# Grouped 3x3 convolution: the distance at which input loads are issued, and wait instructions early on two engines

## The chip, the cores and the metric

The kernel runs on one core of one Trainium2 chip. The metric is the device time of one execution in microseconds (us). Eight executions of the kernel before took 125.8 to 126.14 us, median 125.95. The profile is one further execution of its own; its time stands in the table below.

## The reference

Sixteen images of 64 channels and 64 x 64 pixels are convolved with 3 x 3 filters in 8 groups (8 input and 16 output channels each), with zero padding. Everything is float32 in HBM.

```python
batch, c_in, h, w, c_out, k, groups = 16, 64, 64, 64, 128, 3, 8
x_pad = np.pad(x, ((0, 0), (0, 0), (pad, pad), (pad, pad)))
for g in range(groups):
    for b, co, ci, kh, kw in ...:
        output[b, g * 16 + co] += weight[g * 16 + co, ci, kh, kw] * x_pad[b, g * 8 + ci, kh:kh+h, kw:kw+w]
```

Input: 16.8 MB are read. Output: 16 images of 128 channels, 2.10 MB each, 33.6 MB are written.

## The kernel before

All 16 images go through the same stages, one after the other:

1. *Load.* `load(n)` (line 125) is issued on GpSimd's queue. It reads one image (1.05 MB of float32), casts it to bfloat16 on the way and writes 0.52 MB into slot `n % NX` of the tile `xx`, which has `NX = 8` slots, in the 32 partitions of the middle filter row.
2. *Shift.* `shifted` (line 193, copies at line 198) on VectorE copies these rows twice within `xx`, one image row up and one down, into the 32-partition bands of the two other filter rows. So one product with 96 partitions covers three filter rows.
3. *Products.* `matmuls(n, s)` (line 239, the instruction at line 258) on TensorE: for each half image `s`, three filter columns, four row blocks, two halves of the channels, 24 products into one of the two PSUM tiles `ps`.
4. *Eviction.* `evacuate(n, s)` (line 271, the copy at line 278) on ScalarE copies the PSUM tile into the output buffer `ob[n % 4]`. From image 4 on it first waits until the store that last used this buffer has ended. When an image is whole (in two halves for image 0), SyncE issues its store (line 283).

The order is written out by hand. Each engine has an `Order` object that counts what it has finished on a semaphore; `wait` (line 72) puts a wait into the engine's instruction stream, and `done` (line 83) counts. A wait stands in the stream of its engine, so all that follows it on this engine waits too. The build puts waits of one engine onto the instruction that follows them, or into separate wait instructions ahead of it.

The start is different. The first 36 rows of images 0 and 1 come as float32 through `raw` (the fourth output buffer, line 115, on SyncE's queue) and are cast by ScalarE (three quarters of it) and VectorE (line 207, `cast`), so that the first products needn't wait for a casting load. The weights come on ScalarE's queue (line 118) and are spread by VectorE (line 176), transposed by TensorE (line 183) and masked (line 216) with a mask that GpSimd makes (lines 142 to 152). TensorE runs products on zeros (`spin`, line 160) meanwhile. GpSimd issues loads 0 and 1 first, makes the mask and the identity, then issues loads 2 to 7 at once (line 156).

The main loop (line 286) goes over the images. At its end, for images 0 to 7, GpSimd waits for the last product of image `n` and issues load `n + 8`, which goes to the slot that image `n` used:

```python
        if n + NX < NB:
            POOL.wait(wrote[n, 1])
            load(n + NX)
```

The first memset of VectorE (line 133, `zero`) gives the semaphore value `z`; the next ones follow it at once.

Of the kernel before, what the change touches and what calls it, by code (L numbers as in the profile page):

```python
# [9 lines left out]
ALU = mybir.AluOpType  # L10

NX = 8
NOB = 4
KQ = (1, 0, 2)
ROWS = 36
SPINS = 11, 4, 4, 3, 3


@with_exitstack
def kernel(  # L20
# [16 lines left out]
    t = dict(  # L37
        xx=pool.tile([128, NX, 2, H, W], BF16, name="xx"),
        ob=[pool.tile([128, H * W], FP32, name=f"ob{i}") for i in range(NOB)],
        w_sb=pool.tile([128, CIg * K * K], FP32, name="w_sb"),  # L40
# [8 lines left out]
    with tc.tile_critical():  # L49
        waits = program(nc, x, weight, out, **t)  # L50
# [38 lines left out]
def program(nc, x, weight, out, xx, ob, w_sb, wb, mask4, mask, ident, zero, wt, ps):  # L89
    H = W = 64  # L90
    HW, CIg, COg, R, NB = H * W, 8, 16, 8, 16
    sems = []
    PE = Order(nc, nc.tensor, "pe", sems)
    DVE = Order(nc, nc.vector, "dve", sems)
    ACT = Order(nc, nc.scalar, "act", sems)
# [3 lines left out]
    def sem(name):  # L99
        s = nc.alloc_semaphore(name)  # L100
        sems.append(s)
        return s

    def quad(kh):
        q = KQ.index(kh)
        return slice(32 * q, 32 * q + 32)
# [6 lines left out]
    s_w, s_raw = sem("w"), sem("raw")  # L113
    raw = ob[NOB - 1]
    nc.sync.dma_start(
# [9 lines left out]
    def load(n):  # L125
        s, r0 = sem(f"ld{n}"), ROWS if n < 2 else 0
        nc.gpsimd.dma_start(  # L127
            xx[QC, n % NX, :, r0:, :].rearrange("c s h w -> c s (h w)"),
            x[n].rearrange("(s c) h w -> c s h w", s=2)[:, :, r0:, :].rearrange("c s h w -> c s (h w)"),
        ).then_inc(s, 16)  # L130
        landed[n] = (s, 16)

    z = DVE.done(nc.vector.memset(zero, 0.0))  # L133
# [2 lines left out]
    edge = []  # L136
    for kh, row in ((0, 0), (2, H - 1)):
        e = DVE.done(nc.vector.memset(xx[quad(kh), :, :, row, :], 0.0))  # L138
    load(0)
    load(1)  # L140
    POOL.wait(m1)
# [13 lines left out]
    ))  # L155
    for n in range(2, NX):
        load(n)


    def spin(i, *needs):  # L160
        PE.wait(*needs)
        for _ in range(SPINS[i]):
            spun = nc.tensor.matmul(ps[1][:, 1536:2048], zero[:, 0:128], zero, start=True, stop=True)  # L163
# [29 lines left out]
    def shifted(n, a, b, halves=slice(0, 2)):  # L193

        u = n % NX
        lo, hi = max(a, 1), min(b, H - 1)
        for kh, r0, r1 in ((0, lo, b), (2, a, hi)):
            ins = nc.vector.tensor_copy(  # L198
                xx[quad(kh), u, halves, r0:r1, :].rearrange("c s h w -> c s (h w)"),
                xx[QC, u, halves, r0 + kh - 1 : r1 + kh - 1, :].rearrange("c s h w -> c s (h w)"),  # L200
            )
        return DVE.done(ins)
# [30 lines left out]
    pe = nc.tensor  # L233
    stored = [nc.alloc_semaphore(f"st{i}") for i in range(NOB)]
    uses = [0] * NOB
    free = {0: w_ready}
    wrote = {}

    def matmuls(n, s):
        u = n % NX  # L240
        for kw in (1, 0, 2):
            w0, w1 = max(0, kw - 1), min(W, W + kw - 1)
            v0 = w0 - (kw - 1)
            ws = []
            for half in range(2):
                ws.append(wt[0:96, kw, 64 * half : 64 * half + 64])
            PE.wait(w_ready, e, ready[n, s])
            for c in range(4):
                if kw == 1 and c == 0:
                    PE.wait(free.get(s))  # L250
                for half in range(2):
                    pos = dict(tile_position=(0, 64 * half))
                    r0 = 32 * s + R * c
                    x_ap = xx[0:96, u, half, r0 : r0 + R, w0:w1]
                    o_ap = ps[s][:, 512 * c : 512 * c + 512].rearrange(
                        "p (h w) -> p h w", w=W
                    )[64 * half : 64 * half + 64, :, v0 : v0 + w1 - w0]
                    ins = pe.add_instruction(  # L258
                        mybir.InstMatmult(
                            name=nc.get_next_instruction_name(),  # L260
                            engine=mybir.EngineType.PE,
                            start_tensor_calc=kw == 1, stop_tensor_calc=kw == 2,
                            tile_size=(128, 64), ldweights=c == 0, **pos,
                            ins=[pe.lower_ap(x_ap, opt=False),
                                 pe.lower_ap(ws[half], opt=False, for_matmul_weights=True)],
                            outs=[pe.lower_ap(o_ap)],
                        )
                    )
        wrote[n, s] = PE.done(ins)

    def evacuate(n, s):
        slot = n % NOB
        if n >= NOB:
            ACT.wait((stored[slot], 16 * uses[slot]))
        elif n == NOB - 1:
            ACT.wait(*raw_read)
        ACT.wait(wrote[n, s])
        free[s] = ACT.done(nc.scalar.copy(ob[slot][:, 2048 * s : 2048 * s + 2048], ps[s]))  # L278
        if s == 1 or n == 0:
            o0 = 0 if n > 0 or s == 0 else HW // 2  # L280
            o1 = HW // 2 * (s + 1)
            SP.wait(free[s], (s_warm, 16))
            nc.sync.dma_start(outf[n][:, o0:o1], ob[slot][:, o0:o1]).then_inc(stored[slot], 16)
            uses[slot] += 1

    for n in range(NB):
        if n == 1:
            DVE.wait(raw_read[0])
            ready[n, 0] = shifted(n, 0, 32)
        DVE.wait(landed[n])  # L290
        if n < 2:
            ready[n, 1] = shifted(n, 32, 64)
        elif n == 2:
            ready[n, 0] = shifted(n, 0, 32)
            ready[n, 1] = shifted(n, 32, 64)
        else:
            ready[n, 0] = ready[n, 1] = shifted(n, 0, H)
        for s in range(2):
            matmuls(n, s)
            evacuate(n, s)  # L300
        if n + NX < NB:
            POOL.wait(wrote[n, 1])
            load(n + NX)

    POOL.wait(SP.done(nc.sync.nop()))
    nc.clear_and_free_semaphores(sems)
# [35 lines left out]
```

## Time and profile before

| | |
|---|---|
| time of the runs, median of 8 | 125.95 us |
| time of the profiled execution | 125.94 us |
| span from its first to its last instruction | 123.8 us |
| TensorE, products | 95.6 us busy (77%), 796 instructions |
| VectorE | 77.3 us busy (62%), 51 |
| ScalarE | 66.9 us busy (54%), 36 |
| GpSimd | 15.7 us busy (13%), 23 |
| mean bytes moved | 345 GB/s over the span; HBM read and written together 407 GB/s |
| mean granted TensorE clock | 0.92 |

In the lines of the profile PE is TensorE, DVE VectorE, ACT ScalarE, POOL GpSimd, SP SyncE; a "q" behind a name is the queue of that engine. "L278" is line 278 of the kernel. A group of instructions shows its line, engine and operation, its output and input tiles with their shapes, the count, then busy time and mean nanoseconds of one, then the idle time of the engine just before these instructions and what ended most of it. A wait line shows who waited for whom: us in total, times, the longest. A line of the DMA queues shows packets, megabytes (as written), and the time their packets took as a share of the 16 DMA engines. A line of a stretch shows its length, then busy time and number of instructions of PE, PE's weight loads, DVE, ACT and POOL, then the granted clock, the mean busy share of the DMA engines (it can pass 1, since packets overlap) and the GB/s written. The row of digits named DMA has one digit for each fortieth of the span, 9 for 90% or more busy.

Some times of the start that are referred to below: the raw input is issued at 1.03 us and lands before 7.14, when ScalarE's and VectorE's first casts start; ScalarE's only table load takes 1.28 us from 1.41; the first product on data starts at 11.92; ScalarE's first eviction starts at 14.74.

### The profile page before, as it was taken

The page shows a single profiled execution, that of the slowest core. Times are in us where ns is not written, and L with a number is a line of the kernel's source. Part 1 is how long each engine was busy: PE and PEld are TensorE (multiplying, and loading weights), DVE is VectorE, ACT ScalarE, POOL GpSimd, SP SyncE. Part 2 cuts the span into 40 slices and gives each one's busy share as a digit, 9 for nine tenths or more (in the row PEclk, how much of TensorE's full clock was granted, in tenths as well). Part 3 has the DMA queues.
Part 4 walks back from the last instruction along what each step waited for, and adds up shares of the span by engine and source line. Part 5 has one row for each costly group of instructions (what it writes and reads, how often), then busy time and mean ns, then how long its engine had stood idle before and what let it go on. Part 6 is the DMA issues. An engine that isn't in the chain of part 4 may idle for free.

```text
span 123.8 us, 1252 instructions
## 1 busy us (share of the span) xinstructions
PE 95.6 (77%) x796; PEld 15.7 (13%) x220; DVE 77.3 (62%) x51; ACT 66.9 (54%) x36; POOL 15.7 (13%) x23
## 2 busy tenths in 40 slices
PE   5876999997999938819979994999999999920000
PEld 1231111101111101001111101111111111100000
DVE  4279999999999999999999999980000000000000
ACT  4069677665677356073294719077776777760000
POOL 5910010402031051030070000000000000000000
PEclk9999999999999999995899998599999999995555
DMA  2999999999999999999999999999999999999991
GB/s 34 373 224 212 212 215 241 270 294 299 286 339 379 297 339 339 331 344 357 339 429 429 342 368 440 418 429 424 424 424 434 434 429 424 445 424 440 429 429 48
DMA packets 4052, 42.65 MB, mean 345 GB/s; under 512 B 704, under 2 KB 720, under 8 KB 848
## 3 DMA queue, kind: packets, MB, share of 16 engines
q1 hardware_dynamic: 2624, 34.74, 66.5%
q0 software_dynamic: 1280, 7.80, 30.6%
q10 hardware_dynamic: 144, 0.04, 0.3%
q8 instruction: 4, 0.07, 0.2%
HBM read 16.82 MB, written 33.56 MB: 407 GB/s over the span
## 4 chain that ended last, share of the span: by engine, by line
DMA 41%; PE 37%; ACT 7%; DVE 3%; issue 1%; ACTq 0%; SPq 0%
DMA out_dram<-ob 37%; PE ps L258 35%; ACT ob L278 7%; DMA w_sb<-in_weight_dram 4%; DVE xx L198 2%; PE ps L163 1%; DVE wb L176 0%; DVE wt L216 0%; PE ps L183 0%; ACTq L337 0%; SPq L49 0%
## 5 line engine op out<-in xcount | busy, mean ns | idle before, releaser
L258 PE MATMUL ps<-xx,wt 96*64 96x504 bf16 (+1 forms) x768 | 87.7, 390 | 9.9 <-ACT ob L278 5.9
L278 ACT COPY ob<-ps 128x2048 f32<-128x2048 f32 x32 | 59.3, 1867 | 38.0 <-PE ps L258 19.9
L198 DVE COPY xx<-xx 32x8064 bf16<-32x8064 bf16 (+4 forms) x40 | 73.2, 1831 | 0.9
L258 PEld LDWEIGHTS ps<-xx,wt 96*64 96x64 bf16 x192 | 12.9, 113 | 84.0 <-issue 69.0
L127 POOL DMA_DIRECT2D xx<-in_x_dram x16 | 14.9, 934 | 49.1 <-PE ps L258 48.0
L163 PE MATMUL ps<-zero 128*128 128x512 bf16 x25 | 7.8, 462 | 2.7 <-DVE mask L134 1.5
L207 ACT CAST xx<-ob 32x2304 bf16<-32x2304 f32 x3 | 6.3, 2109 | 4.5 <-DMA ob<-in_x_dram 4.4
L163 PEld LDWEIGHTS ps<-zero 128*128 128x128 bf16 x25 | 2.6, 116 | 6.9 <-issue 2.2
L207 ACT ACT_TABLE_LOAD x1 | 1.3, 1283 | 1.4 <-SPq L49 1.4
L207 DVE CAST xx<-ob 32x2304 bf16<-32x2304 f32 x1 | 1.3, 1347 | 0.9 <-DMA ob<-in_x_dram 0.9
L176 DVE CAST wb<-w_sb 128x96 bf16<-128x96 f32 x3 | 0.6, 254 | 2.0 <-DMA w_sb<-in_weight_dram 2.0
L138 DVE MEMSET xx<- 32x512 uint32 x2 | 1.0, 485 | 0.3 <-issue 0.3
L133 DVE MEMSET zero<- 128x256 uint32 x1 | 0.3, 272 | 1.1 <-SPq L49 1.1
L183 PE MATMUL ps<-ident,wb 128*96 128x128 bf16 x3 | 0.3, 222 | 0.7 <-DVE wb L176 0.7
L170 DVE TENSOR_REDUCE mask<-mask 128x4 f32<-128x16 f32 x1 | 0.2, 180 | 0.7 <-POOL mask L152 0.7
L216 DVE TENSOR_TENSOR wt<-ps,mask 96x384 bf16<-96x384 f32 x1 | 0.6, 554 | 0.0
L183 PEld LDWEIGHTS ps<-ident,wb 128*96 128x96 bf16 x3 | 0.2, 122 | 1.2 <-issue 1.2
L147 POOL TENSOR_SCALAR_AFFINE_SELECT ident<-ident 128x128 bf16<-128x128 bf16 x1 | 0.3, 299 | 0.0
L142 POOL TENSOR_SCALAR_AFFINE_SELECT mask<-mask 128x16 f32<-128x16 f32 x1 | 0.2, 228 | 0.1
L152 POOL TENSOR_SCALAR_AFFINE_SELECT mask<-mask 128x16 f32<-128x16 f32 x1 | 0.2, 215 | 0.0
L323 POOL MEMSET const-float32-0.0<- 128x1 f32 x1 | 0.1, 100 | 0.3 <-issue 0.3
L135 DVE MEMSET ident<- 128x64 uint32 x1 | 0.1, 112 | 0.0
(4 smaller groups left out, 0.4 us busy)
## 6 DMA issues: line engine op xcount, KB each, us to landing
out_dram<-ob SPq DMA_DIRECT2D x15, 2048.0 KB, 18.4
xx<-in_x_dram POOLq DMA_DIRECT2D x14, 512.0 KB, 11.6
out_dram<-ob SPq DMA_DIRECT2D x2, 1024.0 KB, 13.6
ob<-in_x_dram SPq DMA_DIRECT2D x1, 1152.0 KB, 6.1
xx<-in_x_dram POOLq DMA_DIRECT2D x2, 224.0 KB, 6.7
w_sb<-in_weight_dram ACTq DMA_DIRECT2D x1, 36.0 KB, 4.7
out_dram<-in_x_dram SPq DMA_DIRECT2D x1, 8.0 KB, 6.2
```

The costliest lines, as they stand in the source:

```text
L127: nc.gpsimd.dma_start(xx[QC, n % NX, :, r0:, :].rearrange("c s h w -> c s (h w)"), x[n].rearrange("(s c) h w -> c s h w", s=2)[:, :, r0:, ...
L133: z = DVE.done(nc.vector.memset(zero, 0.0))
L138: e = DVE.done(nc.vector.memset(xx[quad(kh), :, :, row, :], 0.0))
L147: m4 = POOL.done(nc.gpsimd.affine_select(out=ident, in_=ident, compare_op=ALU.not_equal, fill=1.0, base=0, channel_multiplier=1, pattern=[ ...
L163: spun = nc.tensor.matmul(ps[1][:, 1536:2048], zero[:, 0:128], zero, start=True, stop=True)
L176: f = nc.vector.tensor_copy(wb[:, :, 32 * q : 32 * q + 32].rearrange("p t (g c) -> p t g c", c=CIg), wv[:, kh].rearrange("p c t -> p t c") ...
L183: ins = nc.tensor.matmul(ps[0][0:96, 128 * kw : 128 * kw + 128], wb[:, kw, :], ident, start=True, stop=True,)
L198: ins = nc.vector.tensor_copy(xx[quad(kh), u, halves, r0:r1, :].rearrange("c s h w -> c s (h w)"), xx[QC, u, halves, r0 + kh - 1 : r1 + kh ...
L207: return order.done(copy(xx[QC, n, half, 0:ROWS, :].rearrange("c h w -> c (h w)"), raw[32 * q : 32 * q + 32, 0 : ROWS * W],))
L216: w_ready = DVE.done(nc.vector.tensor_mul(wt.rearrange("p t (s g c) -> p (t s) g c", s=2, g=4), ps[0][0:96, 0:384].rearrange("p (t g c) -> ...
L258: ins = pe.add_instruction(mybir.InstMatmult(name=nc.get_next_instruction_name(), engine=mybir.EngineType.PE, start_tensor_calc=kw == 1, s ...
L278: free[s] = ACT.done(nc.scalar.copy(ob[slot][:, 2048 * s : 2048 * s + 2048], ps[s]))
```

## The change

Two things are changed. First, in the main loop the load that is issued after image `n` is that of image `n + 5` in place of `n + 8`. It begins with `n = 3` (load 8) and ends with `n = 10` (load 15); loads 0 to 7 are issued as before. The slot of image `n + 5` was last used by image `n - 3`, whose products are over by then. Second, after VectorE's memsets, VectorE executes 40 and ScalarE 90 waits for the first memset, `z`, written directly to the engine. The build puts two waits into one instruction and joins the last of them with the next wait of the program: 20 more instructions on VectorE, ahead of its wait for the mask, and 45 more on ScalarE, behind the issue of the weights' load and ahead of its wait for the raw input.

```diff
 NX = 8
+AHEAD = 5
...
+IDLE = dict(ACT=90, DVE=40)
...
         e = DVE.done(nc.vector.memset(xx[quad(kh), :, :, row, :], 0.0))
+
+
+    for order, times in ((DVE, IDLE["DVE"]), (ACT, IDLE["ACT"])):
+        for _ in range(times):
+            order.eng.wait_ge(*z)
     load(0)
     load(1)
...
-        if n + NX < NB:
+        if NX <= n + AHEAD < NB:
             POOL.wait(wrote[n, 1])
-            load(n + NX)
+            load(n + AHEAD)
```

In the built program ScalarE's table load stands behind the last of these wait instructions, which holds the wait for the raw input as well. In the program before, the table load has no wait ahead of it, and the wait for the raw input is on the first cast.

## Prediction

> **What bounds the kernel now.** I read the slices and the DMA queues of the page first, then the chain of waits, then the DMA answer of single stretches.
>
> ```profile
> DMA  2999999999999999999999999999999999999991
> ...
> q1 hardware_dynamic: 2624, 34.74, 66.5%
> q0 software_dynamic: 1280, 7.80, 30.6%
> q10 hardware_dynamic: 144, 0.04, 0.3%
> q8 instruction: 4, 0.07, 0.2%
> ```
>
> The 16 DMA engines are busy in every slice but the first and the last. The four shares add to 97.6% of the 123.8 us span, 120.8 us. In the DMA answer for 2.0 to 2.5 us the first packets start near 2.05 us, and 2.05 + 120.8 = 122.85 us: nothing is left for idle DMA engines inside the run. q1 carries the stores (and 1.18 MB of raw input at the start), q0 the casting loads. Next, the stretches (columns after the engines: granted clock, DMA share, GB/s):
>
> ```profile
> 8.00:20.00 12.00, 10.22 (x85) 1.55 (x26) 11.71 (x13) 9.27 (x6) 0.53 (x1) 1.00 1.04 212
> 20.00:36.00 16.00, 14.97 (x140) 1.93 (x34) 15.81 (x10) 11.13 (x6) 3.43 (x3) 1.00 1.03 293
> 36.00:62.00 26.00, 20.58 (x176) 2.89 (x42) 25.75 (x12) 11.89 (x7) 4.04 (x3) 0.93 1.02 342
> 80.00:120.00 40.00, 28.93 (x268) 4.67 (x66) 3.19 (x2) 22.40 (x12) 0.00 (x0) 0.88 1.01 431
> ```
>
> The DMA share is 1.01 to 1.04 whether only loads run (8 to 20), both (20 to 62) or only stores (80 to 120). GB/s counts bytes written; a load writes half of what it reads, so 212 written is 424 read, the 431 of the stores again. **The bound is DMA work, and a load costs about its source bytes.** Last, the chain and the waits:
>
> ```profile
> DMA 41%; PE 37%; ACT 7%; DVE 3%; issue 1%; ACTq 0%; SPq 0%
> ```
> ```profile
> ACT ob L278 <- DMA out_dram<-ob: 18.1, 5, 4.8
> ...
> PE ps L258 <- ACT ob L278: 5.9, 4, 3.0
> ```
>
> ScalarE waits 18.1 us for output buffers to be stored, and TensorE waits behind it. TensorE is not the end: its last product starts at 108.5 us, and some 14 us of stores follow. The chain shows TensorE only because it names one predecessor at a time; the DMA row says what runs out.
>
> **Part 1, loads 8 to 15 moved.** Before, load n+8 is issued after the products of image n; now load n+5 is. Load 8 moves from after image 0 (issued at 17.59) to after image 3 (34.37 before), load 15 from after image 7 (62.6) to after image 10. Same eight DMAs, 8.4 MB read, 529 to 2529 ns on GpSimd's queue each, and nothing behind them there but the final wait. SyncE's queue isn't touched. Removed work: 0. Added work: 0. Only idle DMA time, or another cost per byte, can change the end.
>
> *Is a load now late?* A rule speaks against the change: the Trainium skill, DMA: Bandwidth & Descriptors (the table of advice at its end), says to issue a DMA early, compute, and wait late, so that its fixed cost is overlapped. The row that bears on it: loads took 6.4/11.3/20.1 us (min/median/max) from issue to landing, the max being load 7 behind seven others. The new distance leaves four images between issue and need. TensorE does one image in 5.2 us (15.75 us for 144 matmuls, three images), so 20.8 us; VectorE's shifted copies of an image take 2 x 2.25 = 4.5 us, which leaves 16.3 us for a landing of 11 to 13. By the row: 0 us exposed. By the rule as a warning, were each landing to take the max of 20.1, 3.8 us late per image, and the queued stores (two to four of 4.9 us each once loads and stores mix) still cover it. I take 0.
>
> *Does the DMA run dry while loads 8 to 10 are withheld?* This is the real question. From the DMA answers: q0 moved 2.97 MB written up to 20 us and 0.63 MB in 20 to 25; loads 0 to 7 are 3.60 MB, so they are through at about 25 us. In the same 20 to 25 q1 moved 0.75 MB of stores. From 25 us the DMA has stores alone, at 0.43 MB/us:
> - image 0's remaining 2.10 - 0.75 = 1.35 MB: to 28.1 us
> - image 1, issued when its copy ends (22.52 + 1.87 = 24.4): 4.9 us more, to 33.0
> - image 2, issued at 29.6: to 37.9
> - image 3's copy ends at 34.11 + 1.87 = 35.98. The first input load, issued at 1.03, had its first packets at 2.05, so about 1.0 us on an unburdened queue: first packets at 37.0.
>
> So the queue stays fed with 0.9 us to spare before part 2, and load 8 (issued at 34.4, GpSimd 0.5 to 2.5 us, first packets near 36 to 38) arrives just there. Afterwards each image brings 4.9 us of store and about 2.5 us of load per 5.2 us of products: the backlog grows until the four output buffers throttle ScalarE again. No other thin place. If the cover is gone, each us of lateness beyond 0.9 costs about one us at the end, less what load 8 fills.
>
> **Part 2, the waits on ScalarE and VectorE.** All wait for the first memset, done at about 1.4 us; two waits go into one instruction. The price of one is in the trace: 17 ns at ScalarE (13 such, 17/17/38), 21 ns at VectorE. The gap to the next instruction isn't shown; the copies of ScalarE with an extra wait in front start 2.65 us after the one before, those without 2.54, where without any they stood 2.59 apart: some 55 ns each. Between the ends, ScalarE 45 x 17 to 55 ns = 0.8 to 2.5 us, VectorE 20 x 21 to 55 ns = 0.4 to 1.1 us. ScalarE is free from 1.41 to 7.14 (waits for raw input), VectorE from about 2.8 to 5.68 apart from a 0.18 us reduction (waits for the weights, 1.99 us). Hidden at either end: 0. Uncovered it would need over 125 ns an instruction.
>
> What isn't free is where the table load goes. In the built program the wait for the raw input now stands in the last of ScalarE's wait instructions, ahead of the table load; before, the table load stood ahead of that wait. So this moves from under the wait to behind it:
>
> ```profile
> L207 ACT ACT_TABLE_LOAD x1 | 1.3, 1283 | 1.4 <-SPq L49 1.4
> ```
>
> By the row: casts begin at 7.14 + 1.28 = 8.42. The first ends at 10.53; VectorE took it at 10.50, so +0.05 us there, and TensorE's first product at 11.92 becomes about 11.97. The third cast ends at 13.52 + 1.28 = 14.80; VectorE wants it at 14.3, so **+0.5 us** for VectorE, which then has no slack up to image 3 (TensorE waits for it at 28.70). ScalarE's first eviction 14.74 becomes 14.82. Image 3's store and load 8 go 0.5 us later: first packets at 37.5 against the dry point 37.9. Still covered: 0.
>
> By the rule: the Trainium skill, ScalarE: Activation LUTs (What ACT_TABLE_LOAD costs), gives 1283 ns, this row's own number, *plus* a drain of 1380 ns, 2.66 us in all. No row here can show the drain: the next cast came at 7.14, long after. Then the casts begin at 9.80, the first ends at 11.91 (VectorE and TensorE +1.4), the third at 16.2 (VectorE +1.9). Image 3's first packets come at 38.9, 1.0 us after the dry point, and load 8 may fill part. The rule's sum is +0.7 to +1.0 us, the row's 0. Ends 0 and +1.0; I take the row, since the three casts stand back to back here (6.38 us for three of 2.11) and nothing in the trace shows a drain.
>
> **Sum.** 123.8 span + 0 = 123.8; the remainder of the small margins I put at +0.1. The profiled execution took 125.94 us, 2.1 around its span, and the median is 125.95, so no correction: **126.0 us**. Same means within 0.2%, 0.25 us, about what can be told here.
>
> **Rivals.**
> 1. *The DMA runs dry before image 3's store* (slower). One mechanism: table load with its drain after the raw input, VectorE 1.9 us late, image 3's store 1.0 us after the store of image 2 has drained, no load in the queue. It decides once the delay passes 0.9 us. For it: the withheld loads are what filled this stretch before. Against: load 8 may fill it. Time: 125.94 + 0.7 to 1.0 = 126.8. If TensorE's longer gap at 11.3 also costs it the full clock (the clock row shows 0.53 in 56 to 59 after a gap of 3.04 us, but 1.00 after one of 2.38), 3.4 us at half speed adds 1.7 us of delay, up to 127.5.
> 2. *Bytes get cheaper* (faster). In 20 to 36, 293 GB/s of which about 2.07 MB loads and 2.61 MB stores: 2 x 2.07 + 2.61 = 6.75 MB in 16 us, 422 GB/s, against 431 for stores alone. The 11 us from 25 to 36 at stores' rate would win 11 x 2% = 0.2 us, at most 0.45 if the later mix keeps the better rate: 125.6. Against: the loads only mix later, with as many stores.
> 3. *Loads late* (slower): needs landings over 16.3 us for several images and the store backlog used up: each such image costs up to 3.8 us less backlog; about 127.5. The rows speak against it.
> 4. *No effect because the loads aren't later*: the wait for image 3's products is real in before (34.37), so only if TensorE ran ahead; it can't, VectorE holds it at 28.70. Time 126.0, same side as the forecast.
>
> **How the numbers follow.** Forecast 0.46 (126.0, with rival 4 in it; its own range 125.7 to 126.2), rival 1 0.33 (126.8), rival 2 0.16 (125.6), rival 3 0.05. So faster 0.16, same 0.46, slower 0.38. The range 125.5 to 127.0 takes in both ends of the table load and of the byte cost and leaves out rival 3 and the clock.
>
> **What would show it.** Right: DMA share at 1.0 or more in every stretch from 5 to 120, stores alone at about 430 GB/s from 25 to 36, ScalarE's waits for stores far fewer before 60 us and more after 75, table load at 7.1, first cast at 8.4, VectorE never waiting long for a load. Wrong: a DMA share under 0.95 between 33 and 40 us (rival 1), the first cast at 9.8 (the drain), TensorE idle behind a load after 50 us (rival 3), or over 435 GB/s in read and written bytes in the mix (rival 2).

## The result, and the profile after

The changed kernel took 126.81 us (median of 11 runs, 126.48 to 127.44) against 125.94 us before: a ratio of 1.0077, 95% interval 1.0064 to 1.0091. It is slower by 0.77%, about 0.97 us by the means. That is the side and the number of rival 1, not of the case that was held likeliest (126.0, its own range 125.7 to 126.2).

Its profiled execution took 126.5 us with a span of 124.8. So 1.7 us lie around the span, where before had 2.1. The change thus did two things, and they have opposite signs: between the two profiles the span grew by 1.0 us, and the time around it fell by about 0.45. The profiled execution is one of the fastest of the changed kernel, whose mean span is 125.2 us, some 1.4 us above the 123.8 of before; less 0.45 this makes the 0.97.

First the DMA side. These are the row of busy digits, the GB/s of each fortieth of the span (3.1 us), and the queues, from the page of the changed kernel:

```profile
DMA  2999999999999999999999999999999999999990
GB/s 39 367 221 218 210 221 234 289 420 436 441 431 205 376 336 331 373 315 341 344 299 339 341 302 365 420 431 326 394 425 436 425 420 420 425 446 441 420 415 37
...
q1 hardware_dynamic: 2624, 34.74, 65.9%
q0 software_dynamic: 1280, 7.80, 30.9%
...
q14 instruction: 2, 0.02, 0.0%
```

The digits are all 9 as before; they don't show the loss. The GB/s do. After four slices at 420 to 441 (stores alone, as expected once loads are withheld) comes one at 205, from 37.4 to 40.6 us. A mix of loads and stores writes less than stores alone, but the neighbours with as many loads have 299 to 376. The last row above is new: before, q14 had no packets inside the span.

The same stretches as before, of the changed kernel:

```profile
20.00:36.00 16.00, 14.68 (x136) 1.81 (x32) 15.82 (x9) 10.64 (x6) 1.04 (x1) 1.00 1.00 382
36.00:62.00 26.00, 25.39 (x236) 3.71 (x60) 24.82 (x12) 18.30 (x11) 6.48 (x6) 1.00 1.02 336
80.00:120.00 40.00, 27.75 (x240) 4.28 (x58) 7.45 (x4) 19.94 (x11) 0.81 (x1) 0.87 1.01 417
```

The DMA share is 1.00 or more in each of them. TensorE is busier from 36 to 62 us (25.39 us against 20.58), so it runs ahead of the stores, which is worth nothing here. To find the loss I looked at 36 to 42 us alone, as a stretch and by queue (packets, MB written, share of the 16 engines). First the changed kernel:

```profile
36.00:42.00 6.00, 6.00 (x58) 0.84 (x14) 5.94 (x4) 4.30 (x3) 0.75 (x2) 1.00 1.00 284
q0 software_dynamic: 71, 0.51, 53.1%
q1 hardware_dynamic: 89, 1.20, 46.9%
```

Then before:

```profile
36.00:42.00 6.00, 6.00 (x60) 0.80 (x14) 5.96 (x3) 3.73 (x2) 0.57 (x1) 1.00 1.03 347
q1 hardware_dynamic: 97, 1.56, 61.2%
q0 software_dynamic: 80, 0.52, 41.8%
```

The loads moved nearly as much in both; the stores moved 0.36 MB less, 0.84 us at the stores' 0.43 MB/us. The shares say where this time went: the stores had 14.3% of the 6 us less, 0.86 us; the loads took 11.3% more for the same bytes, 0.68 us, and the last 3%, 0.18 us, nobody used. In the core of the dip, 38.5 to 40.5 us, of the changed kernel:

```profile
q0 software_dynamic: 41, 0.34, 112.1%
q1 hardware_dynamic: 3, 0.02, 2.0%
```

Load 8 has the engines to itself for 2 us, though image 3's store was issued at 36.6 us (its copy starts at 34.70 and takes 1.87). And the load is slow: 0.34 MB in 1.12 x 2 us of engine time is 0.15 MB/us, where loads alone between 8 and 20 us in before made 2.54 MB in 1.044 x 12 us, 0.20 MB/us. Only in the next 1.5 us has q1 more, so the store started about 4 us after its issue. From 40.5 to 42 us:

```profile
q1 hardware_dynamic: 24, 0.39, 61.9%
q0 software_dynamic: 14, 0.04, 21.5%
```

These two add to 0.83, and from 37.5 to 38.5 us the share is 0.78: at both ends of the dip the engines were in part idle, which a stretch of 6 us doesn't show.

The start of ScalarE, from the timeline of the changed kernel (start, duration, what, idle before it):

```profile
7.23 1.28 ACT L214 ACT_TABLE_LOAD   x1 [7.23 <-DMA ob<-in_x_dram]
8.53 6.38 ACT L214 CAST xx<-ob 32x2304 bf16<-32x2304 f32 x3
14.91 1.87 ACT L285 COPY ob<-ps 128x2048 f32<-128x2048 f32 x1
```

The table load did move behind the raw input, and the first cast starts at 8.53, straight after it: no drain. Last the waits of the changed kernel that answer to those of before, and VectorE's, which is new:

```profile
ACT ob L285 <- DMA out_dram<-ob: 16.1, 4, 5.8
DVE xx L205 <- DMA xx<-in_x_dram: 10.8, 6, 6.9
...
PE ps L265 <- ACT ob L285: 7.4, 4, 3.7
```

VectorE now waits 10.8 us for loads, but late (from 57 us on by its timeline), when several stores are queued.

### The profile page after: what moved, and what is told of

It is laid out like the page before. It is cut to its first block, busy times and chain, and to the rows that moved or that the text cites. A ratio compares the mean times of both kernels' runs of the same rounds, so it can differ in the third digit from the quotient of the medians.

```text
span 124.8 us, 1317 instructions
## 1 busy us (share of the span) xinstructions
PE 97.6 (78%) x796; PEld 16.0 (13%) x220; DVE 77.2 (62%) x51; ACT 67.0 (54%) x36; POOL 15.4 (12%) x23
## 4 chain that ended last, share of the span: by engine, by line
DMA 41%; PE 22%; ACT 12%; DVE 12%; issue 1%; SPq 0%
DMA out_dram<-ob 36%; PE ps L265 22%; DVE xx L205 11%; ACT ob L285 7%; ACT xx L214 5%; DMA ob<-in_x_dram 5%; DVE xx L214 1%; SPq L344 0%; SPq L51 0%
## 5 line engine op out<-in xcount | busy, mean ns | idle before, releaser
L265 PE MATMUL ps<-xx,wt 96*64 96x504 bf16 (+1 forms) x768 | 88.6, 393 | 9.4 <-ACT ob L285 7.4
L205 DVE COPY xx<-xx 32x8064 bf16<-32x8064 bf16 (+4 forms) x40 | 73.2, 1831 | 12.1 <-DMA xx<-in_x_dram 10.8
L170 PE MATMUL ps<-zero 128*128 128x512 bf16 x25 | 8.9, 514 | 2.4 <-DVE mask L136 1.5
```

Of the source, the lines that this page charges most:

```text
L205: ins = nc.vector.tensor_copy(xx[quad(kh), u, halves, r0:r1, :].rearrange("c s h w -> c s (h w)"), xx[QC, u, halves, r0 + kh - 1 : r1 + kh ...
L265: ins = pe.add_instruction(mybir.InstMatmult(name=nc.get_next_instruction_name(), engine=mybir.EngineType.PE, start_tensor_calc=kw == 1, s ...
```

## The experiments

Theories. T1, *collision*: image 2's store runs out near 37.8 us; load 8 comes into the engines ahead of image 3's store, which then starts late, and the load alone is slow until it does. T2: only the 0.5 us of lateness from the table load opened the gap. T3: loads that mix in later cost more everywhere. T5 and T6, T7 came up on the way. All comparisons are with the kernel before on the same chip.

**Each part alone, and other distances.** Loads five ahead with the waits removed:

```diff
-    for order, times in ((DVE, IDLE["DVE"]), (ACT, IDLE["ACT"])):
-        for _ in range(times):
-            order.eng.wait_ge(*z)
```

> Only the loads are moved (five images ahead); the added wait instructions are gone, so the table load runs at 1.4 us again and image 3's store is issued 0.5 us earlier, near 36.0 us. Theory T1 (collision: when image 2's store has run out near 37.75 us, load 8 is in the DMA engines ahead of image 3's store, whose first packets come 3.5 to 4 us after its issue; the load alone is slow meanwhile, about 1.0 us lost): the order of load and store is the same, so 126.5 to 126.8 us. T2 (it was only the 0.5 us of lateness from the table load): 125.9 to 126.1 us. T3 (loads mixed in later cost more everywhere): 126.8 us and no single dip between 36 and 42 us.

Measured: 1.0059 (1.0034 to 1.0084), mean span 124.9 us against 124.1. The loads alone make most of the loss and T2 falls: with image 3's store issued 0.5 us earlier, at 36.1 us, the dip is still there, and the store's packets start only near 39.5. From 36 to 42 us:

```profile
36.00:42.00 6.00, 6.00 (x58) 0.80 (x14) 5.96 (x3) 3.81 (x3) 0.57 (x1) 1.00 1.01 307
```

The changed kernel has 284 GB/s in this stretch, so the table load may widen the dip, but it doesn't make it.

The waits alone (`AHEAD = 8`):

> Only the added wait instructions; loads eight images ahead as before. The table load stays behind the raw input, VectorE is 0.5 us late up to image 3, but the load queue is full. T1, T2 and T3 all expect the time of before, 125.9 to 126.1 us. If it comes out at 126.4 or more, the waits cost by themselves and all three are incomplete.

Measured: 0.9975 (0.9954 to 0.9995), faster, which no theory had. The mean span is 124.2 us against 124.1; the time around it is 1.73 us against 2.19. This is taken up below.

Six ahead, with the waits (`AHEAD = 6`):

> Waits kept, loads six images ahead. Load 8 is issued near 28.5 us, while the stores of images 1 and 2 are still queued. T1: load 8 mixes with them, the store queue doesn't run dry with a load alone, 125.9 to 126.1 us. T2: the lateness is the same and the thin place is filled, 126.0 us. T3: about two thirds of the loss, 126.5 us.

Measured: 0.9964 (0.9943 to 0.9986), the same as the waits alone, so no cost of the distance of six beside eight can be told. T3 falls: two thirds of the delay gives none of the loss.

Four ahead, with the waits (`AHEAD = 4`):

> Waits kept, loads four images ahead. Load 8 is issued near 40 us, behind image 3's store (36.6 us). T1: no load stands ahead of that store, it follows image 2's store with little or no gap (1.0 us after its issue, against a dry point of 37.75): 126.0 to 126.3 us, faster than five ahead. T2 and a plain shortage of DMA work expect more loss with less work in the queues: 127.0 us or more. T3: 127.1 us.

Measured: 1.0115 (1.0064 to 1.0166). My number from T1 was wrong; the trace shows how. The stretch 36 to 42 us, where the changed kernel has its dip, and the next one, of this kernel:

```profile
36.00:42.00 6.00, 6.00 (x58) 0.87 (x14) 5.94 (x4) 4.55 (x3) 0.57 (x1) 1.00 1.00 426
42.00:48.00 6.00, 6.00 (x58) 0.99 (x14) 5.96 (x3) 4.08 (x3) 2.04 (x1) 1.00 0.95 242
```

Image 3's store, issued at 37.2 us with no load in the engines, did follow image 2's without a gap, as T1 said. But the store queue is short then, one store at a time, and the same meeting takes place one image later: load 8 ahead of image 4's store. I had worked out only the first place. The dip is deeper (share 0.95), which also fits a plain shortage of DMA work, so this run doesn't tell these apart; the next ones do.

**The dip filled in three ways.** Image 3 stored in two halves, all else as changed:

```diff
-        if s == 1 or n == 0:
-            o0 = 0 if n > 0 or s == 0 else HW // 2
+        if s == 1 or n in (0, 3):
+            o0 = 0 if n not in (0, 3) or s == 0 else HW // 2
```

> The changed kernel with image 3 stored in two halves, the first issued near 34.1 us, before the store queue runs out near 37.8 us and before load 8 has packets. T1 (a load alone ahead of a store that finds its queue empty runs slowly until the store starts): the store queue is never empty beside the load, the dip between 38 and 42 us goes; the halves' 8 KB rows cost up to 0.2 us more than whole rows, so 126.0 to 126.3 us, a ratio of 1.000 to 1.003 to before. T5 (a load that starts after the load queue has been empty is slow by itself, whatever the stores do): the dip stays, ratio 1.007 to 1.010.

Measured: 0.9967 (0.9950 to 0.9984). The loads stand where the change put them; only the store queue isn't empty when load 8 comes. From 36 to 42 us the GB/s are 377, and the queues are these:

```profile
q1 hardware_dynamic: 214, 1.96, 77.3%
q0 software_dynamic: 36, 0.29, 23.7%
```

So the loss is not in the loads' lateness, and T5 falls for load 8: it starts after the same pause and moves 0.29 MB in 0.237 x 6 us, 0.20 MB/us. The ratio is 0.003 below the range expected, which had left out what the waits gain.

Load 8 alone issued after image 1, the others five ahead:

```diff
-        if NX <= n + AHEAD < NB:
+        if n == 1:
+            POOL.wait(wrote[n, 1])
+            load(NX)
+        if NX < n + AHEAD < NB:
```

> The changed kernel with load 8 alone issued after image 1 (near 23 us, while the load queue still has load 7); loads 9 to 15 stay five ahead. T1: one load more beside the stores up to 30 us pushes the store queue's end from 37.8 to past 40 us, behind the start of image 3's store; load 9 (40.2 us) then joins a fed store queue: no dip, ratio 0.998 to 1.002. T5: load 9 is now the first after an empty load queue and is slow in its turn, ratio 1.005 to 1.008. T3 (later mixing costs everywhere): 1.006.

Measured: 0.9968 (0.9952 to 0.9985), and 433 GB/s from 36 to 42 us. Load 9 also starts after a pause here, and 42 to 48 us has 362 GB/s with no dip. Seven of the eight loads, moved as in the change, cost nothing; the one that met an empty store queue cost all. (This ratio too is just below its range, for the same reason.)

The kernel before with only the stretch without loads taken over:

```diff
-        if n + NX < NB:
+        if 3 <= n < NB - NX:
             POOL.wait(wrote[n, 1])
-            load(n + NX)
+            for m in range(NX if n == 3 else n + NX, n + NX + 1):
+                load(m)
```

> The kernel before, without added waits, but loads 8, 9, 10 and 11 all issued after image 3 (near 34.4 us); from then on the loads stand eight ahead again. Only the stretch without loads is taken over from the change. T1: the store queue runs out near 37.8 us with loads ahead of image 3's store, so the dip of the change comes back, ratio 1.005 to 1.010. T3: the later mix is that of before, ratio 1.000 to 1.002.

Measured: 1.0063 (1.0042 to 1.0085). The dip is back, 272 GB/s from 36 to 42 us:

```profile
36.00:42.00 6.00, 6.00 (x60) 0.80 (x14) 5.94 (x4) 4.54 (x3) 6.00 (x4) 1.00 0.99 272
q0 software_dynamic: 64, 0.48, 53.8%
```

Four loads were issued one behind the other here, so it doesn't take a load that stands alone in its queue. The rate of the loads (MB written over their engine time) tells the two kinds of kernel apart in all the traces: 0.13 to 0.18 MB/us in the five stretches with a dip (the changed kernel twice, five ahead without waits, this one, and four ahead from 42 to 48 us), and 0.20 to 0.21 from 36 to 42 us in before and in the seven other kernels that load there.

Six ahead without the waits:

> Loads six images ahead, no added waits: the candidate that could beat both. T1: load 8 joins while image 2's store is queued, so no dip; the DMA work is that of before, ratio 0.998 to 1.001. If the 0.996 of six ahead with waits was a real gain of the distance, it shows again here, below 0.998; if the waits gave it (0.9975 alone), it doesn't.

Measured: 1.0008 (0.9986 to 1.0031). So the 0.996 of six ahead came from the waits.

**What the waits do.** The mean time around the span, over the runs that are compared, sorts the kernels: 1.71 to 1.74 us with both groups of waits (the changed kernel, and the runs with the waits alone, six ahead, four ahead, the halves and the early load), 2.19 to 2.25 us without (before, and the three runs without waits). The page shows where it goes. With the waits, q14, a queue that fetches instructions, has two packets of 8 KB inside the span; without, its last two come after the span has ended, at 125.6 and 125.8 us in the trace of before, whose span is 123.8. T6: the waits only lengthen the two instruction streams, so that the last fetch is asked for earlier. T7: it is the moved table load.

The waits ahead of image 12's work, loads eight ahead:

```diff
     for n in range(NB):
+        if n == 12:
+            for order, times in ((DVE, IDLE["DVE"]), (ACT, IDLE["ACT"])):
+                for _ in range(times):
+                    order.eng.wait_ge(*z)
```

> Loads eight ahead as before; the same 45 and 20 wait instructions, but executed ahead of image 12's work instead of at the start. So far each kernel with the waits took 1.7 us around its span and each without 2.2 us, and the two 8 KB instruction fetches of q14 fall inside the span with them, after it without. T6 (the waits only lengthen the two instruction streams, so that the last fetch is asked for earlier): the place doesn't matter, 1.7 us around the span and, with the table load back at 1.4 us, the span of before: 125.7 to 125.8 us, ratio 0.996. T7 (the gain comes from where the waits stand, with the table load moved behind the raw input): 2.2 us around the span, ratio 1.000.

Measured: 0.9967 (0.9949 to 0.9985), 1.73 us around the span against 2.21. The table load is at 1.41 us, and q14 has its two packets inside:

```profile
span 124.6 us, 1317 instructions
...
q14 instruction: 2, 0.02, 0.0%
```

T7 falls. The waits run from 54.6 us on VectorE and from 86.9 on ScalarE here, and the two fetches come at 61 and 92 us, against 20 and 42 us in the changed kernel: they follow the place of the waits, as T6 says.

ScalarE's waits alone (`IDLE = dict(ACT=90, DVE=0)`), loads eight ahead:

> Loads eight ahead; only ScalarE has its 45 wait instructions, at the start. T6: one of the two fetches moves inside the span, the other stays behind it; if both are then waited for together, the time around the span stays near 2.2 us (ratio 1.000 to 1.002), if they come one after the other it falls by about half, to 1.95 us. T7: 1.7 us, ratio 0.997.

Measured: 0.9959 (0.9931 to 0.9987), 1.94 us around the span. One of the two fetches is inside (at 41 us), the other behind the end (126.2 us): half of the gain outside the span.

VectorE's alone (`IDLE = dict(ACT=0, DVE=40)`):

> Loads eight ahead; only VectorE has its 20 wait instructions; the table load stays at 1.4 us. T6: as with ScalarE alone, one fetch inside the span, 1.95 to 2.2 us around it, ratio 0.998 to 1.000. T7: 2.2 us, ratio 1.000, both fetches behind the span.

Measured: 0.9920 (0.9898 to 0.9941), 1.79 us around the span, one fetch inside (21 us) and none seen behind it. Only 6 runs stand in this ratio; it is the fastest of all, ahead of both kernels, with 20 added instructions and the loads as before. 0.42 us of its 0.67 us lie around the span. T6 had expected 1.95 to 2.2 us around the span and a ratio of 0.998 to 1.000, so it missed here: nearly the whole gain is there with one stream lengthened, the two parts (0.27 and 0.42) add to more than both together (0.48), and ScalarE's fetch isn't in this trace at all. That the waits change the time around the span is shown; that the fetches are how they do it fits most of these traces and isn't shown. That the span was shorter too (124.0 us against 124.24 on this chip) I can't explain, and don't count.

The changed kernel again, on the same chip as these three:

> The changed kernel itself, beside the others on the same chip, so that its two parts can be summed. T1 with T6: five ahead without waits gave 1.0059, the waits alone 0.9975, the sum is 1.003 to 1.006; the first measurement gave 1.0077. A ratio above 1.008 would say that the two parts make each other worse (the table load's 0.5 us in front of image 3's store).

Measured: 1.0068 (1.0041 to 1.0095): mean span 125.65 us against 124.24 (+1.41), around it 1.74 against 2.21 (-0.47). The parts apart gave +0.82 and +0.12 in the span. That their sum falls short of 1.41 hints that the table load makes the collision somewhat worse; but the ratio stays under the 1.008 that was set as the sign of it, and the intervals are too wide to settle it.

## Why the prediction was right on the range and wrong on the step

*DMA work as the bound, and its conservation:* right where no dip is. Six ahead, the halves and the early load move all the loads and cost nothing, as counted. The ground given for it was weaker than it looked: packets overlap (shares up to 1.04), so shares that add to almost the whole span don't exclude idle engines. And "another cost per byte", one of the two ways that it named to change the end, was then priced only as a gain (rival 2).

*Table load behind the raw input:* right in place and size. First cast 8.53 us (8.42 by the row, 9.80 by the rule with a drain); image 3's store issued at 36.6 us (36.5 expected). The row was the better guide; the drain of 1380 ns that the Trainium skill adds (ScalarE: Activation LUTs, What ACT_TABLE_LOAD costs) is not in this trace: the load ends at 8.51 us and the cast starts at 8.53.

*The dry point:* right. The prediction had image 2's store end at 37.9 us; the dip begins between 37.5 and 38.5.

*"First packets at 37.0 (37.5)", and the sum of 0 from it:* **this is the step that failed.** I took 1.0 us from issue to first packet from the first transfer of the run, with nothing else in flight, and let load 8 count as cover. In the loaded engines the store took about 4 us, and load 8 was no cover: it stood ahead of the store and ran at three quarters of its rate. The trace of before had the nearer row: image 0's first store was issued at 16.6 us amid loads, and from 16 to 20 us there is no q1, only the loads:

```profile
q0 software_dynamic: 114, 0.80, 103.5%
```

The right term would have been a loss of 0.8 us (the loads alone) to 1.4 us (the whole change) in the span, in place of 0. Rival 1's 126.8 is met by luck: its 0.7 to 1.0 us was for a drain that isn't there and for engines without work, and it too left out the gain of the waits. Its sign, a share under 0.95 between 33 and 40 us, doesn't show (over the whole of it the share is 1.03). Most of the loss was busy engines at low bytes, and only about a fifth of it, in 36 to 42 us, idle ones.

*Waits at 0:* wrong, by some 0.46 to 0.48 us in favour of the change. All my cover was inside the span; I had set "2.1 us around the span" as a constant. Their own price was low too: in the changed kernel's trace the 44 at ScalarE run from 1.4 to 4.7 us, 77 ns apart, the 19 at VectorE from 1.5 to 3.2, some 95 ns apart, against my 17 to 55. The cover held all the same.

*Loads late:* the cost of 0 was right, "VectorE never waiting long" wrong (6.9 us once). The rule of issuing early (the Trainium skill, DMA: Bandwidth & Descriptors, Rules for kernel authors) did speak truly here, but not for the reason it gives, a fixed cost that is overlapped: later landings cost nothing in the runs at six ahead, with the halves and with the early load; issuing load 8 early kept it from meeting an empty store queue.

The two wrong zeros, some +1.4 and -0.48 in the changed kernel, partly cancel. Without the second the total would have come to about 127.3 us, outside the range; so it landed inside by luck: a second miss, unrelated to the first, made up for part of it.

## What to carry to other kernels

When all DMA engines are busy, ask next what they move: bytes per stretch and queue show a loss that the busy share of a long stretch hides. When a source of transfers is delayed, work out which queue runs empty and what stands first in the engines then, and price a start by a transfer that started under load. Split the time into span and what lies around it for every kernel of a comparison; a constant part is an assumption.

## What the runs showed of the hardware

- A store that finds its queue empty while a load has the engines started about 4 us after its issue (36.6 to past 40.5 us in the changed kernel; 16.6 to 20 in before), against 1.0 us for the first transfer of the run, with nothing in flight; meanwhile load 8 ran at 0.15 MB/us written in place of 0.20. With half a store queued the effect was gone. Why the store starts so late and the load slows isn't shown.
- Twenty wait instructions on VectorE took 0.42 us off the time around the span, 45 on ScalarE 0.27, both 0.48 (at the start as well as ahead of image 12), with instruction fetches moving from behind the span into it. That the fetch is the cause fits where its packets stand in most traces; it isn't shown, and the run with VectorE's alone doesn't fit in size.
